# Two gate rows computed as row sums and passed through memory, and plain fp32 products for half of the first weight group of the last MLP

## The chip, the cores and the metric

The kernel runs on one core of one Trainium2 chip. The metric is device time in microseconds (us): from the start of the program to the end of its last instruction. One core has five engines with a queue of instructions each: TensorE (PE in the profile; its weight loads are shown apart as PEld), VectorE (DVE), ScalarE (ACT), GpSimd (POOL) and SyncE (SP), which here only issues transfers between memory and the on-chip buffers. Products are summed up in PSUM, everything else on chip lies in SBUF, and both have 128 partitions.

## The reference

Two layers work on 256 latent tokens behind 256 context tokens, 1,024 wide. Layer 0 mixes tokens by a conformer convolution, layer 1 by an mLSTM that runs over the tokens in both directions; each is followed by a squared-ReLU MLP with 4,096 inner columns. All is fp32. Each layer's vector `c` (for the latent tokens) and `c_ctx` (for the context) gives six rows of 1,024 by one product each with `ada_w`:

```python
sh1, sc1, g1, sh2, sc2, g2 = jnp.split(silu(c) @ ada_w[i] + ada_b[i], 6)

h = layer_norm(ALPHA * h + g1 * mixer(h * (1 + sc1) + sh1), ln1_g[i], ln1_b[i])
u = h * (1 + sc2) + sh2
h = layer_norm(ALPHA * h + g2 * (square(relu(u @ w1)) @ w2), ln2_g[i], ln2_b[i])
```

Only the latent tokens of layer 1 are put out. This study is about layer 1's `g1` (the gate of attention, as the kernel calls the mLSTM) and `g2` (the gate of the last MLP), and about the first product `u @ w1` of the last MLP.

## The kernel before

**Split products.** TensorE multiplies fast in the reduced type fp32r. To keep fp32 accuracy the kernel writes each operand as a high part (fp32r) and a low part (what is left, as fp32r): ScalarE casts the high part (L155), VectorE subtracts it from the plain number (L156). A product is then three: high by high, high by low, low by high (`mm3`, L186 to L190, and `mm3t`, L224 to L226). In the last MLP with its 256 tokens a tile of activations holds [256 high columns | 256 low columns]; a weight's high part is multiplied with all 512 columns, its low part with the first 256 (`wide`, L202, one output tile at a time; `wides`, L213, four output tiles side by side, k-tile by k-tile), and the two halves of the result are added at the end (`joined`, L218 and L219).

**Weights.** Weight tiles of 1 MB (two output tiles or k-tiles) are fetched on SP's queue (L149) into three buffers called `raw` and split into `wh` and `wl` (of the last MLP's later groups `wx`), of which there are four each. Who reads a buffer last sets when the next transfer into it can begin.

**Modulation.** Layer 1's rows are needed in different shapes. Scale and shift are needed by column (channels on partitions). For them the class `AdaV` works on VectorE: a tile of the transposed `ada_w` (256 KB, buffers `ar`, two of them, loaded at L450) is multiplied with the row silu(c), which stands in all partitions (`crow`), and summed along the row in one instruction (L434, shown as two records, the second being the read of the sum). One `step` handles one tile. The gates are needed by row (channels along the free axis, the same in all partitions), and before the change each comes in a way of its own:

- `g1`: `AdaV` loads plain rows of `ada_w` and VectorE adds them up weighted by silu(c), 8 steps for each 512 columns, 16 in all (L442, L444). At the start of attention's output gate, `row` splits both sums, TensorE sums over the partitions by products with a matrix of ones (L461, four matmuls), and VectorE adds the result to the row `G1` (L463), which was loaded with the bias `ada_b`.
- `g2`: `Ada(1, 10, 2)` has TensorE do the product itself in plain fp32, as 32 matmuls in which only 32 output partitions are used (L356), with weights that are loaded for it (two raw tiles of 1 MB and eight tiles `pw` of 256 KB). These matmuls stand in the seam between attention's down projection and the last MLP. VectorE copies the result (L403), it is split, and in the last MLP's second round `gate2` has TensorE spread it over the partitions (L2031, four matmuls).

**The last seam.** Attention's down projection (L224 to L226) ends with the residual of each block of 128 tokens (VectorE, L1902, L1903, L1906), and the norm of its rows (`row_norm`, L1911, L1912, L1916; the rows are scaled at L1924 on ScalarE for the first block, at L1927 on VectorE for the second). Then `turn` transposes the rows on TensorE (L1961, 128x128 each), and `ln1` writes each transposed tile twice, as the high part and as a plain copy (ScalarE L1981; VectorE L1978), from which VectorE makes the low part (L1967, L1983). The last MLP's first group (four output tiles) follows as `wides` with all eight k-tiles (L213), then the second group (L202).

**Attention's decay chain.** The prefix sums of the forget gate go through an exponential on ScalarE (L1579, with the load of its table), VectorE (L1587), a product with a triangular matrix on TensorE (L1603) and one with ones (L1604).

**What sets the order.** The kernel is written as one program. A list scheduler places each instruction in its engine's queue by what it waits for and by priorities; `tc.issue_after` pins one instruction behind another, `tc.high_priority` moves work up or down, `keep_in_program_order` keeps a piece as written. The steps of `AdaV` for `g1` and the MLP's scale and shift are called in three loops of attention (the value projection, whose turns are counted in `vstep`, L1459, and L1493 and L1531); since they wait only for their loads, the scheduler places their instructions well ahead, in the first MLP.

## Time and profile before

| what | value |
|---|---|
| median of 3 runs | 1636.49 us (1636.38 to 1636.56) |
| the profiled execution | 1636.4 us, span 1634.7 us, mean granted TensorE clock 0.999 |
| TensorE busy | 1624.8 us, 8,758 matmul records |
| VectorE busy | 1071.5 us, 2,013 records |
| ScalarE busy | 732.9 us, 1,176 records |
| GpSimd busy | 15.3 us, 67 records |

The span is what the profiler saw between the first and the last instruction; the device time lies 1.7 us above it. In rows of a timeline the first number is the start in us from the beginning of the span, the second the length of the group, then engine, line, operation, what is written and what is read (buffer numbers left out), shapes, and the count; in brackets stands how long the engine was idle before, and what ended that. A plain fp32 matmul leaves two records. Rows of weight loads (PEld) overlap with those of matmuls. In views of groups a row ends with the busy time, the mean of one in ns, and the idle time ahead of them.

### The profile page before, as it was taken

What the parts mean: (1) busy time and instruction counts of PE and PEld (TensorE: products, weight loads), DVE (VectorE), ACT (ScalarE), POOL (GpSimd) and SP (SyncE); (2) the same over time, 40 slices, a digit from 0 to 9 for tenths busy, and PEclk for the clock granted to TensorE, in tenths of its full rate; (3) what the DMA queues carried; (4) which work ended last, traced back from release to release, by engine and by line L of the source; (5) the groups of instructions that cost most, each with busy time, mean ns of one, the idle gap of its engine ahead of it and who ended that gap; (6) DMA issues with size and microseconds to landing.
All of it is one profiled execution on the core that took longest, in us unless ns stands there. A gap on an engine that the chain in (4) does not pass through costs nothing.

```text
span 1634.7 us, 22791 instructions
## 1 busy us (share of the span) xinstructions
PE 1624.8 (99%) x8758; PEld 1352.7 (83%) x8758; DVE 1071.5 (66%) x2013; ACT 732.9 (45%) x1176; POOL 15.3 (1%) x67
## 2 busy tenths in 40 slices
PE   9999999999999999999999999999999999999998
PEld 6675998888888998877787899888888888878887
DVE  7697896886635877862234643453489876786777
ACT  4314763232324585552223532443478654555453
POOL 0000000000000000000000000000000000000001
PEclk9999999999999999999999999999999999999999
DMA  9766323556523078697563622342556565675552
GB/s 359 257 219 245 104 104 135 172 195 213 174 91 142 23 236 258 199 302 229 194 226 139 248 106 103 130 180 104 177 204 229 209 223 206 235 294 182 181 198 85
DMA packets 88124, 306.87 MB, mean 188 GB/s; under 512 B 12844, under 2 KB 31184, under 8 KB 60112
## 3 DMA queue, kind: packets, MB, share of 16 engines
q1 hardware_dynamic: 65552, 289.12, 50.3%
q10 hardware_dynamic: 22464, 16.30, 3.1%
q8 instruction: 69, 1.13, 0.3%
q14 instruction: 39, 0.32, 0.1%
HBM read 287.52 MB, written 17.86 MB: 187 GB/s over the span
## 4 chain that ended last, share of the span: by engine, by line
PE 98%; DVE 1%; ACT 0%; issue 0%; DVEq 0%
PE mm L186 18%; PE mm L189 18%; PE mm L190 18%; PE mm L202 10%; PE mm L226 3%; PE mm L224 3%; PE mm L225 3%; PE cv L226 2%; PE cv L224 2%; PE cv L225 2%; PE fl L356 1%; PE ln L224 1%; PE ln L225 1%; PE ln L226 1%; PE fl L225 1%; PE fl L224 1%
## 5 line engine op out<-in xcount | busy, mean ns | idle before, releaser
L156 DVE TENSOR_TENSOR wl<-raw,wh 128x1024 fp32r<-128x1024 f32 x344 | 419.0, 1222 | 262.8 <-ACT wh L155 260.4
L155 ACT CAST wh<-raw 128x1024 fp32r<-128x1024 f32 x344 | 359.4, 1053 | 455.2 <-PE mm L189 275.3
L189 PE MATMUL mm<-u,wh 128*128 128x512 f32 (+1 forms) x802 | 288.7, 361 | 0.0
L186 PE MATMUL mm<-u,wh 128*128 128x512 f32 (+1 forms) x674 | 239.4, 356 | 0.0
L190 PE MATMUL mm<-u,wl 128*128 128x512 f32 (+1 forms) x674 | 238.2, 355 | 0.0
L189 PEld LDWEIGHTS mm<-u,wh 128*128 128x128 f32 x802 | 151.2, 189 | 23.0 <-issue 0.8
L186 PEld LDWEIGHTS mm<-u,wh 128*128 128x128 f32 x674 | 127.2, 189 | 20.5 <-issue 2.4
L190 PEld LDWEIGHTS mm<-u,wl 128*128 128x128 f32 x674 | 127.1, 189 | 18.5 <-issue 0.8
L186 PE MATMUL mm<-xm,wh 128*128 128x512 f32 x256 | 100.2, 391 | 0.0
L190 PE MATMUL mm<-xm,wl 128*128 128x512 f32 x256 | 99.6, 389 | 0.0
L186 PE MATMUL mm<-hid,wh 128*128 128x512 f32 (+1 forms) x256 | 93.0, 364 | 0.0
L189 PE MATMUL mm<-hid,wh 128*128 128x512 f32 (+1 forms) x256 | 92.8, 362 | 0.0
L190 PE MATMUL mm<-hid,wl 128*128 128x512 f32 (+1 forms) x256 | 92.7, 362 | 0.0
L224 PE MATMUL mm<-wh,xl 128*128 128x512 f32 x208 | 81.4, 393 | 0.0
L225 PE MATMUL mm<-wh,xl 128*128 128x512 f32 x208 | 81.1, 390 | 0.0
L226 PE MATMUL mm<-wl,xl 128*128 128x512 f32 x208 | 80.9, 392 | 0.0
L189 PE MATMUL mm<-qq,wh 128*128 128x272 f32 x256 | 73.9, 289 | 0.0
L186 PE MATMUL mm<-qq,wh 128*128 128x272 f32 x256 | 73.5, 288 | 0.0
L190 PE MATMUL mm<-qq,wl 128*128 128x272 f32 x256 | 73.5, 288 | 0.0
L1382 DVE SCALAR_TENSOR_TENSOR E<-pad,vecs,E 128x512 f32<-128x512 f32 x64 | 47.9, 748 | 19.3 <-ACT E L1380 18.2
L155 ACT CAST hid<-E 128x256 fp32r<-128x256 f32 (+1 forms) x70 | 34.0, 487 | 58.9 <-DVE E L1223 54.8
L156 DVE TENSOR_TENSOR rr<-mm,rr 128x256 fp32r<-128x256 f32 x64 | 27.0, 422 | 50.8 <-ACT rr L155 50.8
(600 smaller groups left out, 3267.4 us busy)
## 6 DMA issues: line engine op xcount, KB each, us to landing
raw<-w SPq DMA_DIRECT2D x64, 1024.0 KB, 4.8
raw<-wo SPq DMA_DIRECT2D x32, 1024.0 KB, 4.9
raw<-ada_w SPq DMA_DIRECT2D x22, 1024.0 KB, 6.4
ar<-adaT_w SPq DMA_DIRECT2D x64, 256.0 KB, 3.0
raw<-wv SPq DMA_DIRECT2D x16, 1024.0 KB, 6.6
raw<-wq SPq DMA_DIRECT2D x16, 1024.0 KB, 4.8
raw<-wk SPq DMA_DIRECT2D x16, 1024.0 KB, 4.8
u<-wqT SPq DMA_DIRECT2D x56, 256.0 KB, 5.4
```

What stands on the lines that cost most here:

```text
L155: c = nc.scalar.copy(hi, src)
L156: lastsub[0] = nc.vector.tensor_tensor(lo, src, hi.bitcast(F32), op=ALU.subtract).ins
L186: a = nc.tensor.matmul(ps, wh, xh, start=start, stop=False)
L189: nc.tensor.matmul(ps, wh, xl, start=False, stop=False)
L190: lastmm[0] = nc.tensor.matmul(ps, wl, xh, start=False, stop=stop).ins
L202: nc.tensor.matmul(o_, w_, x_, start=start and i == 0, stop=stop and i == 15)
L224: nc.tensor.matmul(ps, xh, wh, start=start, stop=False)
L225: nc.tensor.matmul(ps, xl, wh, start=False, stop=False)
L226: return nc.tensor.matmul(ps, xh, wl, start=False, stop=stop).ins
L356: a = mark_unit[0] = nc.tensor.matmul(ps[32 * j:32 * j + 32], cs[:, kt, 14 - 2 * v:46 - 2 * v], blocks[kt], start=first and kt < 4, stop=l ...
L1382: nc.vector.scalar_tensor_tensor(s2_(acc), pad[:, :, k:k + C], V("w_conv", m * QTAP + k), s2_(acc), op0=ALU.mult, op1=ALU.add)
```

## The change

**Gates.** `AdaV` now handles `g1` and `g2` like scale and shift, as row sums over the transposed weights: 64 steps of one kind where there were 32 and 16 of two kinds. When all are done, `gate_rows` writes the 2 x 1,024 sums, which stand by column, with two transfers on ScalarE's queue into a small tensor in memory, `g_dr`; from there they are read back as rows into all partitions (`G1` at attention's gate, `G2` with the other rows of the last MLP). `row`, `fold_r`, `ada_n3` with its loads, `gate2`, L461, L356's last 32 matmuls and L2031 are gone. `ada_n2.step` is called at all 32 places `vstep` instead of at 16 of them, and once more after the last.

**The seam.** Of the first weight group of the last MLP, the two raw tiles are kept, and only the columns of k-tiles 4 to 7 are split (4 x 512 columns instead of 4 x 1,024). For k-tiles 0 to 3, `whole32` multiplies the raw weights with the plain copy of the activations in plain fp32: 4 output tiles x 4 k-tiles x 2 token blocks, 32 products of 128x128x128. `wides` then adds k-tiles 4 to 7, the first of them with the high weights in two matmuls of 256 columns. ScalarE writes the plain copies first and the high parts later, and the low parts of k-tiles 0 to 3 are needed only by the second group.

```diff
-    def wides(pss, ws, rhs):
+    def wides(pss, ws, rhs, k0=0):
         n = rhs[0][0].shape[-1] // 2
-        for kt in range(8):
+        for kt in range(k0, 8):
             for low in (1, 0) if kt == 7 else (0, 1):
                 for ps, w in zip(pss, ws):
-                    w_, x_, o_ = kcol(w, kt)[low], rhs[kt][0], ps
+                    w_, x_, o_ = kcol(w, kt - k0)[low], rhs[kt][0], ps
                     if low:
                         x_, o_ = x_[:, :n], ps[:, :n]
+                    elif kt == k0 > 0:
+                        for sl in (slice(0, n), slice(n, 2 * n)):
+                            nc.tensor.matmul(ps[:, sl], w_, x_[:, sl], start=False, stop=False)
+                        continue
                     nc.tensor.matmul(o_, w_, x_, start=kt == 0 and not low, stop=kt == 7 and not low)
...
+    g_dr = dp.tile([2, D], F32, name="g_dr")
+
+    def gate_rows():
+        for i, u in enumerate((16, 40)):
+            nc.scalar.dma_start(g_dr[i].rearrange("(k p) -> p k", p=P), ada[1][:, u:u + 8, 1])
+
-    ada_n1, ada_n2 = AdaV(1, range(4), (0, 1)), AdaV(1, range(6, 10), (1,), (4, 5))
+    ada_n1, ada_n2 = AdaV(1, range(4), (0, 1)), AdaV(1, (6, 7, 8, 9, 4, 5, 10, 11), (1,), gate_rows)
...
-        if vstep > ET:
-            ada_n2.step()
+        ada_n2.step()
...
-    G1 = rows(qe.tile([P, D], F32, name="G1"), rows_d[0:1])
+    G1 = rows(qe.tile([P, D], F32, name="G1"), g_dr[0:1])
     R = rows_tile()
-    for i in range(2):
-        ada_n2.row(i, G1[:, HF[i]])
...
+    w32 = []
     for g_ in range(2):
         rx = raw_load(w1_1[g_, 0])
-        for m in range(2 * g_, min(2 * g_ + 2, 3 + Z.pre4)):
-            pre1[m] = split_w(rx[:, (m % 2) * 1024:(m % 2 + 1) * 1024])
+        for i in range(2):
+            w32.append(rx[:, i * 1024:(i + 1) * 1024])
+            pre1[2 * g_ + i] = split_w(w32[-1][:, 512:1024])
...
+    def whole32(y, t, f):
+        for m in range(4):
+            a = nc.tensor.matmul(up4[m][:, BLK[t]], w32[m][:, f * P:(f + 1) * P], y[:, f * P:(f + 1) * P],
+                                 start=f == 0 and t == 0, stop=False)
+        return a.ins
...
+    up4 = [psum("mm" if m < 3 else "cv") for m in range(4)]
     tr0 = turn(0, 0)
-    y0 = ln1(tr0, 0, 0, low=False, blocks=range(2))
+    y0 = plain(tr0, 0, tmp("S"))
     tr1 = turn(0, 1, "cv")
     scaled = ln1_rows(1, True)
+    for f in range(3):
+        a = whole32(y0, 0, f)
     with tc.issue_after(roots[0]):
-        ln1(tr0, 0, 0, low=False, y=y0, blocks=(2, 3))
-    ada_unit(units[0])
-    ada_unit(units[1], range(4))
+        high(y0, 0, 0, tr0)
     with tc.issue_after(scaled):
-        lows(y0, 0, 0)
-        ln1(turn(1, 0), 1, 0)
-        tr2 = turn(1, 1)
-        ada_unit(units[1], range(4, 8))
-        ln1(tr1, 0, 1, True)
-        ln1(tr2, 1, 1)
+        with tc.issue_after(a):
+            tr2 = turn(1, 0)
+            tr3 = turn(1, 1, "fl")
+        y1 = plain(tr2, 0, tmp("S"))
+        with tc.issue_after(mark["turned"]):
+            for f in range(3, 4):
+                a = whole32(y0, 0, f)
+        with tc.issue_after(a):
+            for f in range(4):
+                whole32(y1, 1, f)
...
         elif c < 3:
-            if c == 1:
-                gate2()
             rescale(c - 1)
```

**How the order moves.** In the seam, TensorE's queue before the change (`ln` and `cv` are PSUM tiles of transposed rows, `res` the rows, `fl` the gate's sums, `raw` and `pw` the gate's weights, `cs` is silu(c)):

```order
L1961 MATMUL ln_2257_13078<-ident_78,res_1784_10720 128x128 x4
L1961 MATMUL cv_2259_13088<-ident_78,res_1784_10720 128x128 x4
L356 MATMUL fl_2260_13102<-raw_2247_13058,cs_91 32x512 x4
L356 MATMUL fl_2260_13102<-raw_2248_13060,cs_91 32x512 x4
L356 MATMUL fl_2260_13102<-pw_2249_13062,cs_91 32x512
L356 MATMUL fl_2260_13102<-pw_2250_13064,cs_91 32x512
L356 MATMUL fl_2260_13102<-pw_2251_13066,cs_91 32x512
L356 MATMUL fl_2260_13102<-pw_2252_13068,cs_91 32x512
L1961 MATMUL ln_2261_13119<-ident_78,res_1784_10720 128x128 x4
L1961 MATMUL ln_2263_13137<-ident_78,res_1784_10720 128x128 x4
```

and the corresponding place after it, with the changed kernel's line numbers (`S` are the plain copies of a token block's activations, `raw` now the unsplit weights of the MLP, `mm` and `cv` the first group's sums):

```order
L1973 MATMUL mm_2257_13091<-S_2260_13098,raw_2240_13066 128x128
L1973 MATMUL cv_2258_13092<-S_2260_13098,raw_2240_13066 128x128
L1949 MATMUL ln_2262_13129<-ident_78,res_1798_10769 128x128 x4
L1949 MATMUL fl_2263_13134<-ident_78,res_1798_10769 128x128 x4
L1973 MATMUL mm_2255_13089<-S_2260_13098,raw_2235_13056 128x128
L1973 MATMUL mm_2256_13090<-S_2260_13098,raw_2235_13056 128x128
L1973 MATMUL mm_2257_13091<-S_2260_13098,raw_2240_13066 128x128
L1973 MATMUL cv_2258_13092<-S_2260_13098,raw_2240_13066 128x128
L1973 MATMUL mm_2255_13089<-S_2264_13139,raw_2235_13056 128x128
L1973 MATMUL mm_2256_13090<-S_2264_13139,raw_2235_13056 128x128
```

Twelve products of the first block stand between the two pairs of transposes (the last two are seen here), twenty behind the second pair, and k-tiles 4 to 7 follow; before the change four more of L356 follow and then all eight k-tiles.

At the start of attention's output gate, ScalarE's queue before (`wh` and `xl` are high parts, `E` the decay's numbers):

```order
L155 CAST wh_1819_10854<-raw_1818_10852 128x1024
L155 CAST wh_1822_10877<-raw_1818_10852 128x1024
L155 CAST wh_1831_10914<-raw_1830_10912 128x1024
L1579 ACT_TABLE_LOAD
L1579 ACTIVATE E_1816_10815<-E_1817_10816 128x144
L155 CAST wh_1836_10942<-raw_1830_10912 128x1024
L1582 ACT_TABLE_LOAD
```

and after:

```order
L155 CAST wh_1827_10887<-raw_1826_10885 128x1024
L155 CAST wh_1830_10910<-raw_1826_10885 128x1024
L1569 ACT_TABLE_LOAD
L1569 ACTIVATE E_1824_10848<-E_1825_10849 128x144
L155 CAST wh_1839_10947<-raw_1838_10945 128x1024
L1572 ACT_TABLE_LOAD
L1572 ACTIVATE E_1825_10849<-E_1824_10848 128x144
```

The exponential now stands ahead of the third weight cast instead of behind it. On TensorE the triangular product of the same chain stands three matmuls earlier, the products with ones two later.

In the first MLP's down projection, VectorE's queue before (residual updates `x`, low parts `wl`):

```order
L1246 SCALAR_TENSOR_TENSOR x_30_249<-mm_734_4098,ada0_93,x_30_249 128x256 x2
L156 TENSOR_TENSOR wl_752_4231<-raw_750_4228,wh_751_4230 128x1024
L1246 SCALAR_TENSOR_TENSOR x_41_295<-mm_735_4099,ada0_93,x_41_295 128x256 x2
L156 TENSOR_TENSOR wl_754_4261<-raw_750_4228,wh_753_4260 128x1024
L1246 SCALAR_TENSOR_TENSOR x_52_341<-mm_741_4162,ada0_93,x_52_341 128x256 x2
```

and after (L439 is the row sum, its second row the read of the result):

```order
L1231 SCALAR_TENSOR_TENSOR x_30_249<-mm_734_4099,ada0_93,x_30_249 128x256 x2
L156 TENSOR_TENSOR wl_752_4232<-raw_750_4229,wh_751_4231 128x1024
L439 ISA ar_1477_8584,ada1_94<-ar_1477_8584,L_486_2740,vecs_72 128x512
L439 ISA ada1_94 128x1
L439 ISA ar_1495_8669,ada1_94<-ar_1495_8669,L_487_2741,ada1_94 128x512
L439 ISA ada1_94 128x1
L1231 SCALAR_TENSOR_TENSOR x_41_295<-mm_735_4100,ada0_93,x_41_295 128x256 x2
```

Two row sums now stand between a weight's subtraction and the residual updates that follow. Apart from these places and the instructions that are gone, TensorE's order is the same.

## What the change is predicted to do

> **What bounds the kernel now.** I read four views in this order: the busy time of each engine, the shares of the chain that ended last, TensorE's waits over the whole span, and the timeline of each place that the diff touches.
>
> ```profile
> PE 1624.8 (99%) x8758; PEld 1352.7 (83%) x8758; DVE 1071.5 (66%) x2013; ACT 732.9 (45%) x1176; POOL 15.3 (1%) x67
> ...
> PE 98%; DVE 1%; ACT 0%; issue 0%; DVEq 0%
> ```
>
> The first row gives busy time, share and count of each engine, the second the shares of the chain. TensorE works 1624.8 us of the span, so nearly all time is its own work: what leaves its queue is gained, what is added there is lost, and VectorE (66%) and ScalarE (45%) count only where TensorE waits for them. Those waits are few:
>
> ```profile
> PE cv L180 <- DVE ones L139: 1.1, 1, 1.1
> PE fl L461 <- ACT x L1513: 0.2, 1, 0.2
> PE ln L1603 <- DVE E L1587: 0.2, 1, 0.2
> ...
> ```
>
> Each row names who waits, for whom, and for how many microseconds. The first is at the very start and ends on an instruction that stays; the other two lie where the change works.
>
> **The last seam.** Of the seam between attention and the last MLP, these are TensorE's rows (start, length of the group, count):
>
> ```profile
> 1442.57 0.39 PE L226 MATMUL mm<-xl,og 128*128 128x512 f32 x1
> 1442.81 0.60 PE L1961 MATMUL ln<-ident,res 128*128 128x128 f32 x4
> 1443.24 0.60 PE L1961 MATMUL cv<-ident,res 128*128 128x128 f32 x4
> 1443.77 1.92 PE L356 MATMUL fl<-raw,cs 128*32 128x512 f32 x16
> ...
> 1446.65 1.18 PE L1961 MATMUL ln<-ident,res 128*128 128x128 f32 x8
> 1447.75 1.07 PE L356 MATMUL fl<-pw,cs 128*32 128x512 f32 x8
> 1448.75 0.97 PE L213 MATMUL mm<-x,wh 128*128 128x512 f32 x3
> ...
> 1460.06 2.26 PE L202 MATMUL fl<-x,wx 128*128 128x512 f32 x13
> ```
>
> From the first transposes at 1442.81 to the first matmul of the second weight group at 1460.06 are 17.25 us. The first group's eight k-tiles take 1460.06 - 1448.75 = 11.31, or 1.41 each. The change removes the 32 matmuls of L356 and four of the eight k-tiles, and puts in 32 plain fp32 products of 128x128x128. What one of these costs no row shows in this place; the nearest rows are these:
>
> ```profile
> 7.34 0.71 PE L180 MATMUL mm<-ones 128*128 128x128 f32 x4
> ...
> 69.93 1.02 PE L948 MATMUL mm<-A,lt 128*128 128x512 f32 x2
> 70.79 1.02 PE L948 MATMUL mm<-A,tab 96*128 96x512 f32 x2
> ```
>
> ```profile
> 7.34 0.52 PEld L180 LDWEIGHTS mm<-ones 128*128 128x128 f32 x4 [0.41 <-issue]
> ```
>
> A plain fp32 product leaves two records, each with its own weight load. L948's pairs start 70.79 - 69.93 = 0.86 apart with 512 columns: 0.215 per 128 columns, if the price goes by columns. Transposes start four in 1443.24 - 1442.81 = 0.43, 0.108 for one pass of 128 columns, twice which is 0.215 again. L180 has the exact shape, two products in 0.71 with the pipeline's tail; the tail of a 512-column record is about 0.39 - (1442.81 - 1442.57) = 0.15, so one costs up to (0.71 - 0.15) / 2 = 0.28. I take 0.22, near the two rows that agree, and keep 0.215 and 0.28 as bounds. When can they begin and what feeds them?
>
> ```profile
> 1443.44 0.46 ACT L1981 ACTIVATE x<-ln,cb,ca 128x128 fp32r<-128x128 f32 x1 [1.21 <-PE ln L1961]
> 1443.80 0.45 ACT L1981 ACTIVATE S<-ln,cb,ca 128x128 f32<-128x128 f32 x1
> ...
> 1447.32 0.46 ACT L1981 ACTIVATE x<-ln,cb,ca 128x128 fp32r<-128x128 f32 x1 [0.20 <-PE ln L1961]
> ```
>
> ```profile
> 1445.96 1.00 DVE L1927 TENSOR_SCALAR res<-res,mv 128x512 f32<-128x512 f32 x2
> ...
> 1447.68 0.41 DVE L1978 TENSOR_SCALAR x<-cv,ca,cb 128x128 fp32r<-128x128 f32 x1
> 1448.00 0.41 DVE L1978 TENSOR_SCALAR L<-cv,ca,cb 128x128 f32<-128x128 f32 x1
> 1448.32 0.29 DVE L1983 TENSOR_TENSOR x<-S,x 128x128 fp32r<-128x128 f32 x1
> 1448.51 0.29 DVE L1983 TENSOR_TENSOR x<-L,x 128x128 fp32r<-128x128 f32 x1
> ```
>
> ScalarE's plain copy is now its first output, done at 1443.44 + 0.45 = 1443.9, and each next is 0.36 later, faster than four products (0.88) use it up. So the seam runs: first product 1443.95; twelve of them to 1446.6; eight transposes of the second block, whose rows are scaled at 1446.96 as before and of which the last four then wait for little, 1.10 as in the rows 1446.65 to 1447.75, to 1447.7; twenty products to 1452.1 (the second block's copies start at about 1447.3, as ScalarE's last row did, and four products of the first block cover the first one); four k-tiles at 1.41 to 1457.75; 0.1 for the change of matmul kind and for the first of these k-tiles being issued in halves. The second group starts at about **1457.85** instead of 1460.06: **2.2 us** gained (2.4 at 0.215; at 0.28, 32 x 0.06 = 1.9 less, 0.3).
>
> The cover is ScalarE's and VectorE's work on the other four k-tiles. ScalarE has four copies from 1447.3 and then two steps of 0.35 for each k-tile, so the first k-tile's second block is written by 1449.9, the last by 1451.9. VectorE, free at 1446.96, needs 8 x 0.32 and 4 x 0.19 to 1450.3, and one subtraction more for the first k-tile: 1450.6 against the 1452.1 at which TensorE wants it, and 1452.2 against 1456.3 for the last. If that 1.5 us of cover were gone, each microsecond late would be one lost. The splits of the remaining k-tiles' weights (half of each tile's former columns) were done before the seam. Two raw weight tiles are held until 1452.1, so the fourth 1 MB load is issued only then, behind the row loads on SP's queue. What it feeds comes after two output tiles of 16 matmuls, of which 13 took 2.26 in the row at 1460.06, so after about 5.5, at 1463.3: eleven microseconds for a load and its split, where the loads of this stretch took this (issue to landing last):
>
> ```profile
> raw<-w SPq DMA_DIRECT2D x4, 1024.0 KB, 7.5
> ```
>
> **Attention's gate row and last MLP's gate row.** The ones-matmuls that summed these over partitions leave TensorE:
>
> ```profile
> 1173.34 0.63 PE L461 MATMUL mm<-E,ones 128*128 128x512 f32 x2
> 1174.18 0.73 PE L461 MATMUL fl<-E,ones 128*128 128x512 f32 x2 [0.22 <-ACT x L1513]
> 1174.75 0.63 PE L224 MATMUL mm<-wh,xl 128*128 128x512 f32 x2
> ...
> 1515.34 0.39 PE L2031 MATMUL mm<-S,fold_r 128*128 128x512 f32 x1
> ...
> 1516.27 0.39 PE L224 MATMUL ln<-wh,hid 128*128 128x512 f32 x1
> ```
>
> ```profile
> 1174.03 5.01 ACT L155 CAST xl<-raw 128x256 fp32r<-128x256 f32 x16
> ```
>
> The last MLP's four: 1516.27 - 1515.34 = **0.93**, counted whole, since matmuls stand back to back around them (bounds 0 and 0.93). The first four span 1.41 up to 1174.75, but L224 needs the first of ScalarE's casts, which starts at 1174.03 and takes 5.01 / 16 = 0.31 and its way to TensorE: about 1174.5, so **0.2** (0 to 1.4; 1.4 only if the casts move up as well). The rows' way by memory replaces VectorE's 16 accumulating steps and as many loads. No row shows a store of 1,024 single numbers to memory like the two that are added; they stand on ScalarE's queue in the first MLP, where it is busy 30.6 of 92.4 us (below), and are read back at attention's gate, at 1173, so they cost nothing up to tens of microseconds.
>
> **Attention's decay chain.** ScalarE's exponential now stands ahead of a weight cast that waited for memory:
>
> ```profile
> 1191.21 0.39 PE L225 MATMUL mm<-wh,xl 128*128 128x512 f32 x1
> 1191.76 0.49 PE L1603 MATMUL ln<-E,tri 128*128 128x128 f32 x2 [0.17 <-DVE E L1587]
> ```
>
> ```profile
> 1182.32 1.06 ACT L155 CAST wh<-raw 128x1024 fp32r<-128x1024 f32 x1 [1.37 <-DMA raw<-wo]
> 1183.39 1.28 ACT L1579 ACT_TABLE_LOAD   x1
> ```
>
> The chain's inputs come at least the cast's 1.06 and its wait of 1.37 earlier, 2.4 us, against a stall of 0.55 - 0.24 = 0.31 between the two matmuls (0.24 is the step from L226 to its successor). I count **0.3**. The bounds are 0.3 gained and 0.7 lost: the triangular product is also three matmuls earlier (3 x 0.24), and those three no longer cover anything.
>
> **The row sums.** VectorE gets 32 more steps in the first MLP:
>
> ```profile
> 432.60:525.00 92.40, 92.40 (x435) 77.56 (x434) 46.30 (x70) 30.59 (x41) 0.00 (x0) 1.00 0.36 128
> ```
>
> ```profile
> L434 DVE CUSTOM_DVE_ANT_0 ar<-ar,L,ada 128x512 f32<-128x512 f32 x32 | 24.0, 751 | 8.0 <-DMA ar<-adaT_w 7.2
> ```
>
> ```profile
> 458.20 0.88 DVE L1246 SCALAR_TENSOR_TENSOR x<-mm,ada,x 128x256 f32<-128x256 f32 x2 [3.29 <-PE mm L190]
> 463.64 0.88 DVE L1246 SCALAR_TENSOR_TENSOR x<-mm,ada,x 128x256 f32<-128x256 f32 x2 [3.35 <-PE mm L190]
> ```
>
> In the windows row the columns are the stretch, its length, and the busy times of TensorE, its loads, VectorE, ScalarE and GpSimd. VectorE is busy 46.3 of 92.4 us. 32 sums at 0.75 and a read of the result, under 0.1, make 27. Both rows of residual updates come once in 463.64 - 458.20 = 5.44 and waited 3.3 for TensorE: two sums (1.7) fit in such a pause. Cost: **0**; without the cover, a share of 27.
>
> **Sum**: 2.2 + 0.2 + 0.9 + 0.3 = 3.6. The profiled execution took 1636.4 (its span 1634.7), the median of three runs is 1636.49, so both bases give about **1632.8**.
>
> **The rivals.** (A) Plain products at 0.28: for it, L180's own shape; against it, two rows that agree on 0.215. Gain 3.6 - 1.9 = 1.7: 1634.8. (B) The work orders that moved at the start of attention give back 0.7 to 1.5, by the three matmuls named and by casts that the exponential now holds up: for it, TensorE waits there in two of its four waits; against it, the stalls are only 0.2 each. 1633.9. (C) More than counted: the casts at 1174 move up as well, 1.2 more, 1631.6. (D) Slower: the weight load of each fp32 pass doesn't hide behind the pass ahead. At L180 four loads take 0.52, 0.13 each; with 0.108 for the pass that is 0.24 a pass, 0.48 a product, 15.2 for the 32 instead of 7.0: 8.2 more than in the sum, 1641.0. It decides from 0.22 + 3.6 / 32 = 0.33 a product. Against it, PEld is busy 1352.7 us beside a PE busy 1624.8, which fits in a span of 1634.7 only side by side. By the Trainium skill, page "TensorE: Matmul & The Clock Gate", section "The mechanism", weight loads overlap with matmuls in flight only where the row group differs, which products over all 128 rows don't offer, so it speaks for D. By the two busy times, this trace disagrees with that for matmuls in general. (E) Slower: the row sums crowd VectorE in the first MLP. Of a pause of 3.3, two sums leave 1.6, and their loads were waited for 7.2 / 32 = 0.2 each in the row above; from 0.8 each the pause is full, from 0.8 + 3.6 / 32 = 0.9 the whole gain is gone, and 1.0 each would cost 16 x 0.4 = 6.4: 1639.2.
>
> **How the numbers follow.** What a measurement of this kernel can tell from no change is about 0.2%, 3.3 us, so faster means below 1633.2, and the forecast stands just beyond it. Forecast 0.60 (own range 1632.2 to 1633.5), A 0.13, B 0.15, C 0.05, D 0.04, E 0.03. Of the forecast some five sixths lies below 1633.2: 0.50, with C 0.55 faster. The rest of it, A and B make 0.38 the same; D and E 0.07 slower. The range 1631.9 to 1635.0 takes in the forecast, A and B.
>
> **What would show it.** In the changed profile: fp32 products from about 1443.4 on (what lies ahead of the seam gives 0.5), four of them in 0.88; the first matmul of the second group 15.0 after the first transposes instead of 17.25; no wait at the first product of k-tile 4; no gap ahead of the triangular product; residual updates in the first MLP still 5.44 apart. Products at 0.28 or above, a TensorE wait on the low halves, or a step above 5.44 would each make the forecast wrong.

## The result and the profile after

The changed kernel takes 1650.76 us (median of five runs, 1650.10 to 1653.11) against 1636.49: 1.009 times the time before, with a 95% interval of 1.0075 to 1.0105. It is 14.3 us slower; 3.7 us faster was forecast. In the table of experiments further down, one run of late_store is not counted: it took 1667.07 at a mean granted clock of 0.929, against 0.996 to 0.999 in its other nine.

Where it went shows when the same matmul is found in both traces and its start is subtracted (my own subtraction, in us):

| matmul | before | after | after - before |
|---|---|---|---|
| first gate product of layer 0 | 6.34 | 6.59 | 0.25 |
| first MLP, fourth down projection, last product but one ahead of the stall | 519.75 | 520.75 | 1.00 |
| the product behind the stall | 519.99 | 533.17 | 13.18 |
| some 40 matmuls later | 524.78 | 543.73 | 18.95 |
| attention's output gate, first matmul | 1174.75 | 1193.48 | 18.73 |
| output gate, behind the decay chain | 1234.71 | 1252.64 | 17.92 |
| down projection | 1433.69 | 1451.89 | 18.21 |
| second weight group of the last MLP | 1460.06 | 1475.89 | 15.83 |
| last MLP, behind where `gate2` stood | 1516.27 | 1531.17 | 14.90 |

Nearly all of the loss, 18.7 of 18.95, arises between 520 and 544 of the changed kernel's time, in the first MLP; after it the program gains 4.05. That leaves 14.9 at the last matmul; the profiled spans differ by 15.5 (1650.2 and 1634.7), and the other 0.6 lies behind it. TensorE's waits over the whole span point to the same place. What was 0.2 at most, but for the start, now has this at its head:

```profile
PE mm L186 <- ACT hid L155: 13.2, 2, 11.9
...
PE mm L228 <- ACT xl L155: 1.0, 1, 1.0
...
PE ln L1812 <- ACT og L1800: 0.5, 1, 0.5
```

The timeline of the place, TensorE:

```profile
520.98 0.28 PE L190 MATMUL mm<-hid,wl 128*128 128x256 f32 x1
533.17 0.58 PE L186 MATMUL mm<-hid,wh 128*128 128x256 f32 x1 [11.92 <-ACT hid L155]
534.07 0.58 PE L189 MATMUL mm<-hid,wh 128*128 128x256 f32 x1 [0.31 <-DVE hid L156]
...
537.80 0.58 PE L186 MATMUL mm<-hid,wh 128*128 128x256 f32 x1 [1.23 <-ACT hid L155]
...
543.73 0.37 PE L190 MATMUL mm<-hid,wl 128*128 128x256 f32 x1
```

It waits for one cast of hidden values on ScalarE. ScalarE, SyncE and VectorE there (rows of ACTq and SPq are issues of transfers by ScalarE and SyncE):

```profile
517.01 0.37 ACTq L1257 DMA_DIRECT2D g_dr<-ada  x1
...
531.47 1.14 ACT L155 CAST u<-raw 128x512 fp32r<-128x512 f32 x2 [10.05 <-DMA raw<-w]
532.51 0.61 ACT L155 CAST hid<-E 128x512 fp32r<-128x512 f32 x1
```

```profile
518.74 0.33 SPq L149 DMA_DIRECT2D raw<-w  x1
```

```profile
517.51 1.21 DVE L156 TENSOR_TENSOR wl<-raw,wh 128x1024 fp32r<-128x1024 f32 x1
```

The hidden values' cast stands in ScalarE's queue behind two casts of the last 1 MB weight tile of this MLP, and that tile comes late for two reasons. It is issued at 518.74, when VectorE's subtraction (517.51 + 1.21 = 518.72) releases its buffer; before the change the load was issued at 507.45:

```profile
507.45 0.33 SPq L149 DMA_DIRECT2D raw<-w  x1
```

And it takes 12.6 us from issue to landing. Of the transfers issued between 518 and 532 and between 490 and 545 the trace gives (median us from issue to landing last):

```profile
raw<-w SPq DMA_DIRECT2D x1, 1024.0 KB, 12.6
```

```profile
g_dr<-ada ACTq DMA_DIRECT2D x1, 4.0 KB, 10.9
```

The second row is one of the two added stores of 1,024 single numbers: 4 KB in 10.9 us, issued at 517.01, just ahead of the weight load. The bytes moved between 518 and 532, in 40 slices of 0.35 us, show what the load waits for:

```profile
GB/s 7 4 0 0 0 0 0 0 70 0 0 47 94 94 94 0 47 23 23 47 94 23 23 23 23 0 70 47 23 70 164 374 421 445 445 421 328 375 445 468
```

Up to 527.9, when the store lands (517.01 + 10.9), no slice has more than 94. Nearly all bytes of the loads under way come after it, and this load lands at 531.3.

Why VectorE is late is in its waits between 430 and 545, after the change and, in the second fence, before it:

```profile
DVE ar L439 <- DMA ar<-adaT_w: 28.7, 14, 6.2
```

```profile
DVE ar L434 <- DMA ar<-adaT_w: 2.4, 1, 2.4
```

VectorE now stands 28.7 us in line for the row sums' own loads. The longest of these waits, 6.2, stands behind the other store, which is issued at 470.17. The row of VectorE, and the landing of the three sums' loads and of the store itself among the transfers issued between 470 and 484:

```profile
484.31 0.75 DVE L439 CUSTOM_DVE_ANT_0 ar<-ar,L,vecs 128x512 f32<-128x512 f32 x1 [6.25 <-DMA ar<-adaT_w]
```

```profile
ar<-adaT_w SPq DMA_DIRECT2D x3, 256.0 KB, 8.8
g_dr<-ada ACTq DMA_DIRECT2D x1, 4.0 KB, 11.0
```

Over the whole program the sums' loads take 3.1 in the median, so the first store had a part in VectorE's lateness too; how large it is shows in late_store below.

Behind the stall TensorE runs at half clock. In the windows rows the third figure from the end (ahead of DMA share and GB/s) is the granted clock:

```profile
520.00:533.20 13.20, 0.91 (x4) 0.51 (x4) 3.61 (x5) 3.15 (x6) 0.00 (x0) 0.63 0.72 159
533.20:544.00 10.80, 9.26 (x40) 8.67 (x41) 5.98 (x12) 3.02 (x5) 0.00 (x0) 0.50 0.52 195
544.00:600.00 56.00, 56.00 (x466) 55.72 (x466) 42.02 (x108) 26.24 (x50) 0.80 (x9) 1.00 0.13 45
```

So the 18.7 are about 15.1 of waiting and 3.6 of slow matmuls (18.95 - 13.18 = 5.77 behind the stall, less 0.77 and 1.41 of further waits).

The other places went about as forecast; each is set against its term further down. The seam:

```profile
1460.97 0.60 PE L1949 MATMUL ln<-ident,res 128*128 128x128 f32 x4
1461.41 0.60 PE L1949 MATMUL cv<-ident,res 128*128 128x128 f32 x4
1462.12 0.94 PE L1973 MATMUL mm<-S,raw 128*128 128x128 f32 x6
...
1463.11 0.83 PE L1973 MATMUL mm<-S,raw 128*128 128x128 f32 x6
...
1464.01 0.83 PE L1973 MATMUL mm<-S,raw 128*128 128x128 f32 x6
...
1470.16 0.96 PE L215 MATMUL mm<-x,wh 128*128 128x256 f32 x6
...
1475.89 2.96 PE L202 MATMUL fl<-x,wx 128*128 128x512 f32 x16
```

The second group starts 1475.89 - 1460.97 = 14.92 after the first transposes, against 17.25; four plain products take 1464.01 - 1463.11 = 0.90.

### The profile page after: what moved, and what is told of

The parts are those of the page before. It is cut to its first block, busy times and chain, and to the rows that moved or that the text cites. A ratio compares the mean times of both kernels' runs of the same rounds, so it can differ in the third digit from the quotient of the medians.

```text
span 1650.2 us, 22844 instructions
## 1 busy us (share of the span) xinstructions
PE 1624.0 (98%) x8754; PEld 1356.7 (82%) x8754; DVE 1077.2 (65%) x2052; ACT 728.3 (44%) x1173; POOL 15.2 (1%) x67
## 5 line engine op out<-in xcount | busy, mean ns | idle before, releaser
L156 DVE TENSOR_TENSOR wl<-raw,wh 128x1024 fp32r<-128x1024 f32 (+1 forms) x344 | 416.3, 1214 | 254.3 <-ACT wh L155 251.9
L155 ACT CAST wh<-raw 128x1024 fp32r<-128x1024 f32 (+1 forms) x344 | 356.8, 1045 | 451.0 <-PE mm L189 268.3
L186 PEld LDWEIGHTS mm<-u,wh 128*128 128x128 f32 x674 | 127.2, 189 | 20.5 <-issue 2.4
L186 PE MATMUL mm<-hid,wh 128*128 128x512 f32 (+1 forms) x256 | 95.1, 372 | 13.2 <-ACT hid L155 13.2
L189 PE MATMUL mm<-hid,wh 128*128 128x512 f32 (+1 forms) x256 | 94.8, 370 | 0.7 <-DVE hid L156 0.7
L186 PEld LDWEIGHTS mm<-hid,wh 128*128 128x128 f32 x256 | 50.1, 196 | 21.5 <-ACT hid L155 13.9
```

The lines of the kernel that those rows point to most:

```text
L155: c = nc.scalar.copy(hi, src)
L156: lastsub[0] = nc.vector.tensor_tensor(lo, src, hi.bitcast(F32), op=ALU.subtract).ins
L186: a = nc.tensor.matmul(ps, wh, xh, start=start, stop=False)
L189: nc.tensor.matmul(ps, wh, xl, start=False, stop=False)
```

## The experiments

Two explanations of the stall stood against each other: the **row sums** make the weight load late (theories 1 and 4 in the expectations), and the **stores** of single numbers make it slow (theory 2). All times are medians in us; the kernel before was run beside each group.

| run | time (range) | before, same chip | ratio (95% interval) |
|---|---|---|---|
| the changed kernel | 1650.76 (1650.10 to 1653.11) | 1636.49 | 1.0090 (1.0075 to 1.0105) |
| late_store | 1640.49 (1635.51 to 1643.12) | 1637.07 | 1.0015 (1.0005 to 1.0025) |
| contig_store | 1634.99 (1634.21 to 1639.03) | 1637.07 | 0.9992 (0.9983 to 1.0001) |
| sums_other_queue | 1662.63 (1659.12 to 1666.20) | 1637.07 | 1.0155 (1.0139 to 1.0172) |
| sums_late | 1639.66 (1638.39 to 1640.59) | 1637.07 | 1.0015 (1.0006 to 1.0025) |
| stores_only | 1638.78 (1638.03 to 1639.93) | 1636.75 | 1.0012 (1.0002 to 1.0021) |
| sums_split | 1636.20 (1634.19 to 1637.11) | 1636.75 | 0.9994 (0.9984 to 1.0003) |
| seam_old | 1640.12 (1637.36 to 1640.91) | 1636.75 | 1.0018 (1.0009 to 1.0028) |
| sums_loops | 1632.82 (1632.13 to 1634.11) | 1636.84 | 0.9977 (0.9968 to 0.9985) |
| loops_column_store | 1639.07 (1638.39 to 1639.45) | 1636.84 | 1.0013 (1.0004 to 1.0022) |
| stores_only_contig | 1632.49 (1631.47 to 1633.18) | 1636.84 | 0.9973 (0.9963 to 0.9984) |
| loops_seam_old | 1638.65 (1637.48 to 1640.03) | 1636.86 | 1.0008 (0.9998 to 1.0018) |
| column_loads | 1631.78 (1631.69 to 1632.26) | 1636.86 | 0.9965 (0.9952 to 0.9978) |

In all of them TensorE's order is that of the changed kernel, except in the two with the old seam and in sums_split, where some products between 641 and 744 change places.

### The stores moved, recut, or with the sums' loads on another queue

**late_store** pins the two stores behind a later cast:

```diff
-            nc.scalar.dma_start(g_dr[i].rearrange("(k p) -> p k", p=P), ada[1][:, u:u + 8, 1])
+            with tc.issue_after(mark['st']):
+                nc.scalar.dma_start(g_dr[i].rearrange("(k p) -> p k", p=P), ada[1][:, u:u + 8, 1])
...
+        if vstep == 8:
+            mark['st'] = loaded[1]
```

> The changed kernel with its two column stores moved from the first MLP to attention's value projection (ScalarE's queue, some 270 instructions later); TensorE's, VectorE's and SyncE's orders are the same. Theory 1 (the 32 added row sums are enough: their loads hold up the weight loads behind them on SyncE's queue, and the store only stretches what is late already): the last weight load is still issued near 518.7, lands in about 5 us instead of 12.6, TensorE resumes near 525.6 instead of 533.2, and the clock drops less or not at all: 1638 to 1643. Theory 2 (the stores of single numbers are the whole cause, the sums cost nothing): no stall in the first MLP, 1632.6. Theory 3 (the store has no part in it): 1650.8 as the changed kernel.

Measured: 1640.5. In the first MLP only one wait of 1.4 is left. VectorE's order is that of the changed kernel, so this run shows what the sums do there with no store beside them. VectorE's waits for their loads between 430 and 545, and the last weight load:

```profile
DVE ar L440 <- DMA ar<-adaT_w: 18.2, 13, 3.3
```

```profile
511.75 0.33 SPq L149 DMA_DIRECT2D raw<-w  x1
```

The load lands in 4.8. Theory 1 had expected it near 518.7, as in the changed kernel. So of the 11.3 us by which it is late there, the sums alone make 4.3 (511.75 - 507.45), and the other 7.0 come with the first store.

A new wait stands where the stores now are (issued at 727.5 and 731.1). TensorE's wait, and ScalarE's in the stretch from 735 to 760:

```profile
PE mm L187 <- ACT wh L155: 3.3, 1, 3.3
```

```profile
ACT E L1380 <- DMA xc_dr<-E: 8.8, 1, 8.8
```

ScalarE waits 8.8 us for another store of its own queue to finish, and the weight casts stand behind it. So the stall moved with the stores, and little of it stayed with the sums: theory 2 gains, although the time lies in theory 1's range.

**contig_store** turns the columns on VectorE first:

```diff
-        for i, u in enumerate((16, 40)):
-            nc.scalar.dma_start(g_dr[i].rearrange("(k p) -> p k", p=P), ada[1][:, u:u + 8, 1])
+        nc.vector.transpose(g_t, ada[1][:, 16:48, 1])
+        for i in range(4):
+            nc.scalar.dma_start(g_dr[:, i * 32:i * 32 + 32], g_t[i * 32:i * 32 + 32, :])
```

> The changed kernel with the gate columns turned by one 32x32 block transpose on VectorE, so that memory gets four stores of 32 pieces of 128 bytes instead of two of 1,024 single numbers, at the place of the later of the two stores. If the number of pieces makes the store slow (theories 1 and 2): as late_store, 1638 to 1643 by theory 1, 1632.6 by theory 2. If a store at this place is slow however it is cut: about 1650.

Measured: 1635.0. This is the changed kernel with 128 pieces of 128 bytes where 2,048 pieces of 4 bytes were: 15.8 faster, between the two theories' numbers. The profiled execution took 1639.03, the longest of the ten, so its trace shows more than the median loses. TensorE's waits in the first MLP, and a row of ScalarE:

```profile
PE mm L186 <- ACT hid L155: 3.3, 2, 2.3
```

```profile
516.86 1.05 ACT L155 CAST wh<-raw 128x1024 fp32r<-128x1024 f32 x1 [3.26 <-issue]
```

Half clock for 6.8 us follows, and 6.9 us are lost there. These waits are not the sums' alone: ScalarE stands 3.3 us with issuing the four stores before it goes on with its casts. The last weight load is issued at 512.37, close to late_store's 511.75.

**sums_other_queue** issues the sums' loads from GpSimd:

```diff
-            nc.sync.dma_start(w, adaT_w[self.units[n], kt // 2, kt % 2])
+            nc.gpsimd.dma_start(w, adaT_w[self.units[n], kt // 2, kt % 2])
```

> The changed kernel with the loads of all row sums issued on GpSimd's queue instead of SyncE's, so that no weight load stands behind one of them; the stores of single numbers stay in the first MLP. Theory 1 (queueing on SyncE is the first cause): the weight loads are issued as soon as their buffer is free, some 10 us earlier, the store only eats into the slack: 1632.6 to 1636. Theory 2 (the stores are the whole cause): a load is still stretched by the store, TensorE waits 5 to 8 us: 1640 to 1646.

Measured: 1662.6, worse than all. The two weight loads issued next behind the stores, at 474.86 and 522.07, take 14.2 and 13.4 us to land. VectorE waits longer for the sums' loads between 430 and 560 than the changed kernel did between 430 and 545:

```profile
DVE ar L439 <- DMA ar<-adaT_w: 38.4, 18, 9.2
```

The weight loads no longer stood behind the sums' loads in SyncE's queue, and TensorE still stalled, so that queue is not needed for the stall. What is left of theory 1 is VectorE's waiting in line (theory 4). The scheduler also placed VectorE's work differently here, so why this run is 11.9 us slower than the changed kernel stays open.

**sums_late** holds the sums back by their loads:

```diff
-            nc.sync.dma_start(w, adaT_w[self.units[n], kt // 2, kt % 2])
+            with tc.issue_after(loaded[0]) if self.done and n >= 4 else nullcontext():
+                nc.sync.dma_start(w, adaT_w[self.units[n], kt // 2, kt % 2])
```

> The changed kernel with the 32 added row sums (those of the two gates) held back by their loads until attention's value projection and query and key loops, which puts the two stores there too (ScalarE's queue at instructions 712 and 817 instead of 281 and 305). Both theories say that the stall of 12 us in the first MLP and the low clock behind it vanish. What is left is the gain worked out before: 1636.5 - 3.9 = 1632.6. If attention cannot take the sums or the stores either, above 1634.

Measured: 1639.7, where both theories had said 1632.6. The first MLP is clean, but one sum waits for its load ahead of a subtraction that TensorE needs. VectorE, and TensorE's wait:

```profile
906.14 0.75 DVE L439 CUSTOM_DVE_ANT_0 ar<-ar,L,vecs 128x512 f32<-128x512 f32 x1 [4.74 <-DMA ar<-adaT_w]
...
906.82 2.77 DVE L156 TENSOR_TENSOR xc<-raw,xc 128x256 fp32r<-128x256 f32 x8
```

```profile
PE mm L202 <- DVE xc L156: 3.8, 3, 3.5
```

So a sum costs not by its 0.75 us but by the load that it waits for, with work behind it in VectorE's queue.

### One cause at a time

**stores_only** and **stores_only_contig** leave the 32 added sums out and keep the stores at their places in the first MLP (they write other columns); the diff shown is that of stores_only, and stores_only_contig has the four stores of contig_store instead, at the later place:

```diff
-        for i, u in enumerate((16, 40)):
-            nc.scalar.dma_start(g_dr[i].rearrange("(k p) -> p k", p=P), ada[1][:, u:u + 8, 1])
...
-    ada_n1, ada_n2 = AdaV(1, range(4), (0, 1)), AdaV(1, (6, 7, 8, 9, 4, 5, 10, 11), (1,), gate_rows)
+        for i, u in enumerate((0, 8)):
+            with tc.issue_after(gpin[i]):
+                nc.scalar.dma_start(g_dr[i].rearrange("(k p) -> p k", p=P), ada[1][:, u:u + 8, 1])
...
+    ada_n1, ada_n2 = AdaV(1, range(4), (0, 1)), AdaV(1, (6, 7, 8, 9), (1,), gate_rows)
```

> The changed kernel without the 32 added row sums and their loads; two stores of 1,024 single numbers stand at the two places in ScalarE's queue in the first MLP where the changed kernel has them, and write other columns (so the two gate rows are left out of the computation: wrong numbers take their place). Theory 2 (the store alone is the cause): TensorE still waits 8 us or more in the first MLP: above 1640. Theory 4 (the store only hurts because the row sums have eaten the slack of the weight loads; VectorE stands 28.7 us waiting for the sums' own loads between 430 and 545): the loads are early, the stores fall into their slack, no wait in the first MLP: 1632.6 to 1633.5.

> stores_only (no added row sums; the gate rows again hold other numbers) with the four stores of 32 pieces of 128 bytes instead of the two of 1,024 single numbers, at the same place in the first MLP. If the number of pieces is what costs: no wait there, 1632.6, against stores_only's 1638.8 (2.0 above the kernel before). If any store at this place costs: 1637 to 1639.

Measured: 1638.8 and 1632.5, 6.3 apart. This pair is the cleanest view of the store. In stores_only the store is issued at 504.31 and the last weight load at 507.30, and the load's casts begin at 519.91; between 504.3 and 520 the transfers took (last figure):

```profile
519.91 1.14 ACT L156 CAST u<-raw 128x512 fp32r<-128x512 f32 x2 [6.14 <-DMA raw<-w]
```

```profile
raw<-w SPq DMA_DIRECT2D x1, 1024.0 KB, 12.5
...
g_dr<-ada ACTq DMA_DIRECT2D x1, 4.0 KB, 11.6
```

and in stores_only_contig, with its load issued at 507.38:

```profile
513.75 1.14 ACT L156 CAST u<-raw 128x512 fp32r<-128x512 f32 x2
```

```profile
raw<-w SPq DMA_DIRECT2D x1, 1024.0 KB, 5.2
g_dr<-g_t ACTq DMA_DIRECT2D x4, 4.0 KB, 4.9
```

With the sums gone the load is early and still comes late: the store alone makes 5.2 us into 12.5. Theory 4's 1632.6 for stores_only is refuted. Theory 2's place and mechanism hold, but not its size: TensorE waits 3.9 there where 8 or more were expected, and 1638.8 lies under its bound of 1640.

**column_loads** adds to stores_only_contig two loads of 1,024 single numbers at those two places:

```diff
+        for i in range(2):
+            with tc.issue_after(gpin[i]):
+                nc.scalar.dma_start(g_c[:, 8 * i:8 * i + 8], rows_d[i].rearrange("(k p) -> p k", p=P))
```

> stores_only_contig (no added row sums, contiguous store, wrong numbers in the gate rows) with two loads of 1,024 single numbers each from memory into an unused tile, at the two places in ScalarE's queue in the first MLP where stores_only has its stores. If the many 4-byte pieces are what slows the weight load, whichever way they go: as stores_only, a load of 12 us and about 1638 to 1639. If only writes of 4 bytes do it: no wait, 1632.5.

Measured: 1631.8; no wait. The loads of 4-byte pieces land in 2.4:

```profile
g_c<-rows_d ACTq DMA_DIRECT2D x1, 4.0 KB, 2.4
```

As many pieces of 4 bytes, but read instead of written, are done in 2.4 us where the store takes 11.6, and nothing is disturbed. It is the writing of 4-byte pieces to memory that lasts. What such a read does to a load beside it the run does not show: the second one had landed (504.71 + 2.4 = 507.1) before the weight load went out at 507.70.

### The sums where they cost nothing

**sums_split** gives the sums four buffers in turn, two of them free only in attention, with the contiguous store:

```diff
-            w = adp.tile([P, 512], F32, tag="ar", name=nm("ar"), bufs=2)
+            w = tmp("S") if self.done and n >= 4 and self.i % 2 else adp.tile([P, 512], F32, tag="ar", name=nm("ar"), bufs=2)
```

> The changed kernel with the contiguous store of contig_store, and with every second load of the added row sums in one of two other buffers that the first MLP leaves unused (so that four buffers serve them, not two); since these buffers come free only in attention, 16 of the 32 added sums stay in the first MLP and 16 go to attention's value projection, at the place of the accumulating steps of the kernel before. Theory 4: with half the sums the weight loads of the first MLP keep their slack: no wait of TensorE there and none new, 1632.6. If any sum in the first MLP costs (half of contig_store's 3.3): 1634 to 1635.

Measured: 1636.2; the profiled execution, 1634.85, is one of the shorter ones. The first MLP has no wait there; between 706 and 729, behind the sums that moved, where the convolved features are made and VectorE has its own work, the matmuls fall 2.0 further behind those of the kernel before. A plain miss: that place has no room for the sums either.

**sums_loops** places each sum behind the weight split that stands before it in the program, with its load up to three ahead; it takes over the four buffers of sums_split, the hold on the loads of sums_late and the contiguous store:

```diff
-            if self.i < DT * len(self.units):
+            while self.i < DT * len(self.units) and len(self.loads) < (3 if self.done and n >= 4 else 1):
                 self.loads.append(self.load())
...
+                with tc.issue_after(lastsub[0]) if self.done and n >= 4 else nullcontext():
                     nc.vector.tensor_tensor_reduce(...)
```

> The changed kernel with the contiguous store, and with the 32 added row sums held back (each sum behind the weight split that stands before it in the program, its load up to three ahead in four buffers) so that they stand in attention's query and key loops, behind the split of the convolved features, where VectorE is about half idle. Theory 4 (sums cost only where their loads arrive late in VectorE's queue or where the weight loads have no slack): no wait of TensorE is added anywhere, all of the worked-out gain shows: 1632.6, 4 below the kernel before. If sums cost wherever they are: above 1634.

Measured: **1632.8**, below both kernels (0.9977 of before, 0.9968 to 0.9985). Of the groups of VectorE between 830 and 1175, the last figure is the idle time ahead of them:

```profile
L440 DVE CUSTOM_DVE_ANT_0 S<-S,L,ada 128x512 f32<-128x512 f32 x16 | 11.9, 745 | 0.0
L440 DVE CUSTOM_DVE_ANT_0 ar<-ar,L,vecs 128x512 f32<-128x512 f32 x16 | 11.8, 745 | 0.0
```

The same 32 sums, never waiting for a load: the time is within 0.3 of stores_only_contig, which has no added sums, so nothing shows that they cost. Contig_store, where they stand in the first MLP, is 2.2 slower; its stores stand elsewhere too.

**loops_column_store** is sums_loops with the two stores of single numbers:

> As sums_loops, but with the two stores of 1,024 single numbers instead of the contiguous one, now in the key loop (ScalarE's queue at instructions 747 and 837). Theory 2b (such a store slows every load in flight for some 10 us, and costs wherever a load is wanted within that time): the loads of this loop are three buffers ahead, so 0 to 2: 1632.6 to 1634.6; if it always stalls TensorE by the 5 of stores_only: 1637 to 1638.

Measured: 1639.1, 6.2 slower than sums_loops, above both forecasts. The second store goes out at 1168.88, when attention's output gate begins to fetch its weights. ScalarE, in this run and, in the second fence, in sums_loops:

```profile
1168.88 0.37 ACTq L1259 DMA_DIRECT2D g_dr<-ada  x1
...
1183.76 1.99 ACT L155 CAST wh<-raw 128x1024 fp32r<-128x1024 f32 x2 [4.32 <-DMA raw<-wo]
```

```profile
1178.87 1.99 ACT L155 CAST wh<-raw 128x1024 fp32r<-128x1024 f32 x2
```

The same cast is 4.9 later, 0.5 of it from before the store. The other store, at 1029.9 in the key loop, leaves no wait behind, nor do those of sums_late, at 972.4 and 1133.8. So such a store costs where a transfer that it slows is wanted within some 15 us (1183.76 - 1168.88 here, 519.91 - 504.31 in stores_only): at the end of the first MLP, in the value projection and at the gate's beginning, but not in the key loop.

### The plain products undone

**seam_old** (on sums_split) and **loops_seam_old** (on sums_loops) put the old seam back, without the 32 gate matmuls:

```diff
-    w32 = []
...
-    for f in range(3):
-        a = whole32(y0, 0, f)
...
+            pre1[m] = split_w(rx[:, (m % 2) * 1024:(m % 2 + 1) * 1024])
...
+        ln1(turn(1, 0), 1, 0)
+        tr2 = turn(1, 1)
+        ln1(tr1, 0, 1, True)
+        ln1(tr2, 1, 1)
```

> sums_split with the plain fp32 products undone: the last seam as before the change (all eight k-tiles as split products behind the splits of the activations), but without the 32 gate matmuls that stood in it. By the prediction's rows the first k-tile cannot start before the second block's rows are scaled, turned and split, about 5.9 after the first transposes as before, so the second weight group starts 17.2 after the first transposes, less perhaps 0.5, against 14.9 with the plain products: 1.8 to 2.3 slower than sums_split. Rival: the gate matmuls set the old seam's length, and without them it is as short as the new one: within 0.5 of sums_split.

> sums_loops (the undisturbed version) with the plain fp32 products undone: the old seam without the gate matmuls, as in seam_old. By the prediction's rows (first k-tile not before the second block is scaled, turned and split; second group about 17 after the first transposes against 14.9): 1.8 to 2.3 slower than sums_loops, 1634.6 to 1635.1. By seam_old's trace, in which the seam was 3.9 longer than in sums_split: 1636.7.

Measured: 3.9 slower than sums_split, and 5.8 slower than sums_loops, twice and three times what I had expected. TensorE in loops_seam_old:

```profile
1443.05 0.60 PE L1951 MATMUL ln<-ident,res 128*128 128x128 f32 x4
...
1447.23 1.08 PE L1951 MATMUL ln<-ident,res 128*128 128x128 f32 x8 [3.14 <-DVE res L1920]
1449.08 1.65 PE L217 MATMUL mm<-x,wh 128*128 128x512 f32 x3 [0.77 <-DVE x L1973]
...
1463.19 1.07 PE L202 MATMUL fl<-x,wx 128*128 128x512 f32 x4
```

The seam is 1463.19 - 1443.05 = 20.14 long against 14.92. With neither gate matmuls nor plain products TensorE has nothing to do until the second block's rows are scaled, waits 3.9 (3.14 + 0.77), and the trace's clock record has half clock for 6.8 us from 1448.5 on. The plain products are worth not the difference to the old seam but all of the cover that the gate matmuls used to give.

## Why the prediction was wrong

The forecast was 1632.8; the measured 1650.76 lies far outside the range. The terms of the sum, by their steps:

- **Last seam**, 2.2 predicted: 17.25 - 14.92 = 2.3. A plain product costs 0.22 (0.90 for four), not L180's 0.28, so rivals A and D fall. With two records each, that is 0.11 a record, no more than a transpose's 0.108, so nothing is left for weight loads that don't overlap. The Trainium skill's sentence that weight loads overlap with matmuls in flight only where the row group differs (page "TensorE: Matmul & The Clock Gate", section "The mechanism", which also names a background weight buffer to load into) does not hold for these full products.
- **Attention's gate row**, 0.2: 18.95 - 18.73 = 0.2.
- **Decay chain**, 0.3: 0.8 gained by 1234, of which 0.3 is given back by 1434; on the way TensorE now waits 0.5 for ScalarE's `og`, the gated output. Rival B, which had a loss here, is wrong.
- **Last MLP's gate row**, 0.9: 15.83 - 14.90 = 0.9.
- **The stores**, "they cost nothing up to tens of microseconds": the first step that failed. I asked who waits for the store (nobody for 650 us) and not what it does to the loads in flight. By the pair stores_only and stores_only_contig they cost 6.3 by themselves.
- **The row sums**, "Cost: 0": the second step that failed. I set 27 us of work against 46 us of idle VectorE, and the loads' waits at 0.2 each from a stretch with other work around it. Measured, the waits are 28.7 over 33 sums, 0.87 each, which is rival E's own point of decision (0.8 to 0.9). But part of that is the first store's doing: in late_store, without a store beside them, they are 18.2, or 0.55 each. E had the mechanism, and its chance of 0.03 was too low. Its price was of another kind: not 0.4 per turn, but one late buffer at the end, a wait of 1.4 in late_store.
- **The two together**: 6.3 and 1.4 do not make 18.7. The weight load's issue moved by 11.3 us (507.45 to 518.74). The sums alone make 4.3 of that, by late_store; the other 7.0 come with the first store, which held back the sums' loads and let VectorE wait 6.2 at once. That used up the load's slack and put it right behind the second store, where it took 12.6 instead of late_store's 4.8; the resulting wait of 12 us then cost half clock. That they add up to more than their sum follows from this chain; no run separates how much of the 18.7 each link contributes.

With both mended, sums_loops gives 1632.8, 4.0 less than the kernel before beside it, and the changed kernel gains 4.05 behind the first MLP, where the sum had 3.6: the rest of it stands. That the time equals the forecast to the tenth is luck, since the decay chain did not come out as counted.

## What to carry to other kernels

A transfer that nobody waits for is not free: ask which loads are in flight with it, and do not write a column to memory number by number where it can be turned on the chip; one block transpose and stores of 128-byte pieces took the 6.3 us of stores_only away. Work that waits for loads is held back by such a store too, and then delays what stands behind it. Idle time of an in-order engine is no room for an instruction that waits for a load of its own: what counts is what stands behind it in the queue, and whether its loads run far enough ahead. Where filler work is taken out of a seam, find out what it covered, for its replacement may be worth that cover and not the difference.

## What the runs showed of the hardware that was not expected

- A store of 4 KB as 1,024 pieces of 4 bytes lands in 9 to 12.5 us (20.3 for late_store's second, issued 3.6 us behind its first). A 1 MB load that is issued 1.7 to 3 us behind it takes 12.5 or 12.6 instead of 4.7 to 5.2; it lands 3.4 and 3.9 us after the store does (after: 517.01 + 10.9 and 518.74 + 12.6; stores_only: 504.31 + 11.6 and 507.30 + 12.5). 1,024 reads of 4 bytes land in 2.4. Four stores of 32 pieces of 128 bytes land in 4.9 in stores_only_contig, where the load behind them takes 5.2, and in 6.4 in contig_store, where ScalarE stands 3.3 us issuing them. The Trainium skill, page "DMA: Bandwidth & Descriptors", section "Rules for kernel authors", says that a last dimension that is not contiguous becomes one descriptor per element; the trace agrees with 1,040 packets for one such store. The same page of the Trainium skill, section "Specifications", says that below 512 bytes the engine reads, modifies and writes. That fits a price that only writes pay, but the 128-byte pieces are below that too, and which of size and number of pieces decides was not tried.
- The price of a wait goes on after it. The clock records of the traces show TensorE at half clock for 3.4 us in sums_late (after a wait of 3.5) and 6.8 in stores_only and loops_seam_old, and in the changed kernel, with its wait of 12 us, from 523.4 to 543.9, 20.5 us. All are multiples of 3.41, which agrees with the window of about 3.4 us that the Trainium skill states (page "TensorE: Matmul & The Clock Gate", section "What's actually happening").
